# Feed-forward, second products: every engine in program order, casts a chunk ahead, border work over three chunks, side work in smaller pieces

## Chip, cores and metric

One NeuronCore of a Trainium2 chip runs the whole kernel. The metric is device microseconds (us) of one execution. The engines are TensorE (PE, matmuls; PEld are its weight loads), VectorE (DVE), ScalarE (ACT), GpSimd (POOL) and SyncE (SP, which issues nearly all transfers here). Each engine works through its own instructions in order and waits for others by semaphores.

## What is computed

One layer of a transformer-like block on 2048 tokens of width 1024, in fp32: attention and a gated branch, merged, and then the channel part that the change is about:

```python
    h2 = modulate(x, norm2_g[l], sh2, sc2)
    x = x + g2 * sq_relu_mlp(h2, w_ff1[l], w_ff2[l])

def sq_relu_mlp(h, w1, w2):
    return jnp.square(jax.nn.relu(h @ w1)) @ w2
```

The hidden width is 4096. The gate `g2` is 1024 columns of `silu(c) @ w_mod + b_mod`.

## The kernel before

Every fp32 product is made of three reduced matmuls: each operand is split into a high part h (a cast to fp32r by ACT) and a low part l (the value less its high part, by DVE), and `product` issues h·h, h·l and l·h (L1453, L1454, L1455), each 128x128 weights on 512 columns. The two big products of the feed-forward are in addition cut in two by two blocks and made by seven block products instead of eight (Strassen in Winograd's form), with sums formed by DVE.

The channel part comes last, in four stages; a block is 1024 tokens:

- `ff1` of block 0 (until about 2134 us): 16 groups of hidden columns. Each group makes seven products into PSUM banks, then ReLU and square by ACT (L1466, L1467), then the sums for the second product by DVE (L1463). The seven results of a group are stored to DRAM (`ao_d`), 256 KB each. Beside them `w2_ops` forms the seven sums of the second weights and stores them too (`w2o_d`, L1446).
- `ff2` of block 0 (about 2134 to 2463 us), the stage of the change: seven products p in the order 0, 1, 5, 6, 4, 2, 3, each in 8 chunks (NCH) of the hidden width. A step (p, c) is 24 matmuls: 4 token tiles (TT, one PSUM bank each) by 2 slots by 3. `ff2_chunk` loads a chunk of `ao_d` and one of `w2o_d` (512 KB each, L1542), lets ACT cast both (L1543) and DVE subtract (L1544); it is called two steps ahead of use.
- `ff1` and `ff2` of block 1 (to the end), alike, without `w2_ops`.

At the last chunk of a product, the **border**, `take` empties each bank: copies to SBUF by ACT (L1583, L1590), or `leave`: DVE multiplies with g2 and adds the residual (both through `tt`, L1556), and a later step issues the store to the output. For p = 1, ACT then writes an older sum back into the banks (L1586), since the next product adds onto it.

Beside `ff2` of block 0 runs **side work**, one piece per step: first the gate g2 (`mod_part`: 16 loads of weights, 16 DVE operations L364, L368, two matmuls L380), then `h_ops` for block 1, which prepares its `ff1` operands: load and scale a block of x (L1314, 128x2048 on DVE), 16 transposes by PE (L189), ACT scaling from PSUM (L1324), casts and subtractions (`halves`, L1298, L1299) and sums.

The order on an engine is not the program's. A scheduler reorders instructions by its costs and priorities, within the dependencies. `order` adds dependencies that hold some ranges: for `pins` every engine keeps program order, for `fixed` PE and DVE, for `loads` SP alone. Tiles of a tag are always given out in program order:

```python
            held = idx in pinned or (idx in fixed and i.engine in engines)
            held = held or (idx in loads and i.engine == self.nc.sync.engine)
```

Tags: b4 has 12 buffers of 512 KB, hb 35, f2 16 and f8 2. Before, a chunk takes four b4 buffers, so three chunks fit.

Of the kernel before, what the change touches and what calls it, by code (L numbers as in the profile page):

```python
# [11 lines left out]
F32R = mybir.dt.float32r  # L12
I32 = mybir.dt.int32
AF = mybir.ActivationFunctionType
ALU = mybir.AluOpType
# [4 lines left out]
P = 128  # L20
D = 1024
KC = D // P
# [8 lines left out]
TB = 512  # L31
# [20 lines left out]
def f32(ap):  # L52
    return ap.bitcast(F32)
# [17 lines left out]
class Kern:  # L71
# [280 lines left out]
    def mod_part(self, alloc, names):  # L352
        nc, I = self.nc, self.I
        for what in names:
            at = 2 * D + ("g1", "sh2", "sc2", "g2").index(what) * D
            for n in range(2):
                lo, sl = at + n * TB, slice(n * TB, (n + 1) * TB)
                acc = alloc()
                for k in range(KC):
                    w = alloc()  # L360
                    nc.sync.dma_start(w, I["w_mod"][0, k * P : (k + 1) * P, lo : lo + TB])
                    s = self.silu[:, k, 0:1]
                    if k == 0:
# [45 lines left out]
                yield  # L409

    def rope_consts(self):
        nc, I = self.nc, self.I
# [886 lines left out]
        nc.vector.tensor_tensor(out=l, in0=raw, in1=f32(h), op=ALU.subtract)  # L1299
        return h, l  # L1300

    def x1_block(self, blk, r, kk):
        nc, n = self.nc, 2 * TT
        x = self.sb("f8", [n, 2, P])
        for i in range(2):
            src = self.x1_d[2 * blk + i].rearrange("(t p) c -> p t c", p=P)
            for j in range(2):
                k = kk + j * HK
                nc.sync.dma_start(
                    x[:, i * TT : (i + 1) * TT, j], src[:, :, k * P : (k + 1) * P]  # L1310
                )
        xv = x.rearrange("p t j c -> p t (j c)")
        rb = r.unsqueeze(2).broadcast_to([P, n, 2 * P])
        nc.vector.tensor_tensor(out=xv, in0=xv, in1=rb, op=ALU.mult)  # L1314
        return x

    def x1_turned(self, x, kk):
        nc, raw = self.nc, {}
# [44 lines left out]
    def h_ops(self, blk, ops):  # L1363
        n = 2 * TT
        r = self.rsqrt(self.ss2[:, blk * n : (blk + 1) * n], n, 1.0 / D)
        add, sub = ALU.add, ALU.subtract
        tt = self.nc.vector.tensor_tensor
        for kk in range(HK):
# [145 lines left out]
    def ff1(self, blk, h, extra, w=None, late=()):  # L1514
# [5 lines left out]
        for g in range(NG):  # L1520
            nxt = iter(())
            if g + 1 < NG:
                w[g + 1] = {}
                nxt = self.w1_ops(g + 1, w[g + 1])
            else:
                self.ready = [self.ff2_chunk(blk, 0, 0)]
            more = extra(g)
            for _ in self.ff1_group(blk, g, w.pop(g), h):
                next(late, None)
# [4 lines left out]
            for _ in more:  # L1534
                pass

    def ff2_chunk(self, blk, p, c):
        nc = self.nc
        out = []
        for src in (self.ao_d[blk][p][c], self.wo_d[p][c]):  # L1540
            l, h = self.sb("b4", [2, TB], F32R), self.sb("b4", [2, TB], F32R)
            nc.sync.dma_start(f32(l), src.rearrange("s p c -> p s c"))  # L1542
            nc.scalar.copy(h, f32(l))  # L1543
            nc.vector.tensor_tensor(out=l, in0=f32(l), in1=f32(h), op=ALU.subtract)  # L1544
            out.append((h, l))
        return out

    def ff2(self, blk, side):
        nc = self.nc
        add, mult = ALU.add, ALU.mult  # L1550
        ready = self.ready + [self.ff2_chunk(blk, 0, 1)]
        begin = self.here()
        late = []

        def tt(out, in0, in1, op):
            nc.vector.tensor_tensor(out=out, in0=in0, in1=in1, op=op)  # L1556

        goes = {1: (0, 0), 4: (1, 1), 2: (0, 1), 3: (1, 0)}
        u2, u3, xs = ([None] * TT for _ in range(3))

        def residual(p):
            i, j = goes[p]
            for t in range(TT):
# [3 lines left out]
                    self.x1_d[2 * blk + i][t * P : (t + 1) * P, j * TB : (j + 1) * TB],  # L1567
                )

        def leave(p, t, src):  # L1570
            i, j = goes[p]
            row = (2 * blk + i) * TB + t * P
            cs = slice(j * TB, (j + 1) * TB)
            c = self.sb("f2", [TB])
            tt(c, src, self.g2b[:, cs], mult)
            tt(c, c, xs[t], add)
            late.append(lambda: nc.sync.dma_start(self.out[0, row : row + P, cs], c))

        def take(p, t):
            ps = banks[p][t]  # L1580
            if p == 0:
                u2[t] = self.sb("f2", [TB])
                nc.scalar.copy(u2[t], ps)  # L1583
            elif p == 1:
                leave(p, t, ps)
                nc.scalar.copy(ps, u2[t])  # L1586
            elif p in (5, 6):
                u = u2 if p == 5 else u3
                u[t] = self.sb("f2", [TB])
                nc.scalar.copy(u[t], ps)  # L1590
            elif p in (4, 2):
                u = u3[t] if p == 4 else u2[t]
                tt(u, u, ps, add)
                leave(p, t, u)
            else:
                leave(p, t, ps)

        order = (0, 1, 5, 6, 4, 2, 3)
        steps = [(p, c) for p in order for c in range(NCH)]
        banks = {}  # L1600
        for n, (p, c) in enumerate(steps):
            if n + 2 < len(steps):
                ready.append(self.ff2_chunk(blk, *steps[n + 2]))
            for f in late:
                f()
            late.clear()
            (ah, al), (wh, wl) = ready.pop(0)
            fresh = p in (0, 4)
            if c == 0 and fresh:
                new = [self.bank([TB]) for _ in range(TT)]  # L1610
                for other in (0, 1, 5, 6, 3) if p == 0 else (4, 2):
                    banks[other] = new
            if c == NCH - 1 and p in goes:
                residual(p)
            for t in range(TT):
                tok = slice(t * P, (t + 1) * P)
                a = [(ah[:, s, tok], al[:, s, tok]) for s in range(2)]
                b = [(wh[:, s], wl[:, s]) for s in range(2)]
                self.product(banks[p][t], a, b, fresh and c == 0)
                if c == NCH - 1:  # L1620
                    take(p, t)
            next(side, None)
        for f in late:
            f()
        for _ in side:
            pass
        self.loads.append(range(begin, self.here()))

    def ffn(self, h, w, w1, late):
        for _ in w1:  # L1630
# [6 lines left out]
        side = chain(self.mod_part(lambda: self.sb("f2", [TB]), ("g2",)), self.h_ops(1, h))  # L1637
        self.ff2(0, side)
        self.ff1(1, h, lambda g: iter(()))
        self.ff2(1, iter(()))  # L1640
# [449 lines left out]
```

## Time and profile before

| | before |
|---|---|
| median of 3 runs | 3111.57 us (3110.06 to 3111.89) |
| profiled execution | 3096.51 us, its span 3094.7 us |
| mean granted TensorE clock | 0.987 |
| PE, DVE, ACT, POOL busy | 2991.8, 2062.1, 1465.5, 688.6 us |
| HBM traffic | 172 GB/s over the span |

The profiled execution is 15 us shorter than the median of the runs. Busy time of PE counts pipelined matmuls with modelled ends, so a busy PE still may run slower than at full clock; the granted clock stands beside it for that. A row of the waits names what came last before an instruction could start. A timeline row has the start, the time taken, the engine (SPq is SP's queue), the line, the operation, and in brackets the idle time before it and what ended that.

### The profile page before, as it was taken

To read this page: it belongs to the slowest core of one execution; us is meant where nothing else is said; L and a number is where in the kernel's file an instruction comes from. 1 tells how busy PE (TensorE), PEld (TensorE's weight loads), DVE (VectorE), ACT (ScalarE), POOL (GpSimd) and SP (SyncE) were. 2 spreads that over 40 slices of the span, in tenths; PEclk is the share of its full clock that TensorE was granted. 3 is DMA by queue.
4 is the path that set the end of the run, shared out by engine and by line. 5 is a ranking of instruction groups with operands and counts; after the bars stand their busy time and mean duration, and the time that the engine had idled before them with its cause. 6 is when DMAs were issued, how large, how long until landed. Compare 5 with 4: busy or idle time off the path is not lost.

```text
span 3094.7 us, 37963 instructions
## 1 busy us (share of the span) xinstructions
PE 2991.8 (97%) x13501; PEld 2253.6 (73%) x13501; DVE 2062.1 (67%) x2918; ACT 1465.5 (47%) x2296; POOL 688.6 (22%) x506
## 2 busy tenths in 40 slices
PE   7999999979999999999999989999999999999999
PEld 4877788866555555556877878887777788888777
DVE  4776577866887777678654488776665566654445
ACT  5646664654554545554222255444454344444433
POOL 0000000002898888885234300000000000000000
PEclk8999999989999999999999999999999999999999
DMA  8686766643110000005855459887766644445665
GB/s 298 204 264 215 233 194 202 195 151 118 38 38 22 14 15 14 5 22 189 277 187 174 141 170 322 308 303 270 252 217 219 207 147 150 152 161 196 205 211 203
DMA packets 385726, 534.32 MB, mean 173 GB/s; under 512 B 32048, under 2 KB 203232, under 8 KB 385536
## 3 DMA queue, kind: packets, MB, share of 16 engines
q1 hardware_dynamic: 375760, 515.88, 50.3%
q10 hardware_dynamic: 9776, 16.01, 1.4%
q8 instruction: 106, 1.74, 0.2%
q14 instruction: 84, 0.69, 0.1%
HBM read 367.69 MB, written 164.10 MB: 172 GB/s over the span
## 4 chain that ended last, share of the span: by engine, by line
PE 78%; DMA 8%; DVE 6%; ACT 4%; issue 3%; POOL 1%; SPq 0%; DVEq 0%; ACTq 0%; POOLq 0%
PE b L1454 13%; PE b L1455 13%; PE b L1453 12%; PE b L1982 8%; PE b L1949 5%; PE b L1968 4%; PE b L1914 3%; PE a L1453 3%; PE b L183 3%; PE b L185 3%; PE a L1455 3%; PE a L1454 3%; PE b L184 3%; PE b L189 2%; DMA bw<-in_w_br_gm 1%
## 5 line engine op out<-in xcount | busy, mean ns | idle before, releaser
L1544 DVE TENSOR_TENSOR b<-b,b 128x1024 fp32r<-128x1024 f32 x224 | 272.9, 1223 | 241.1 <-ACT b L1543 236.3
L1925 DVE TENSOR_REDUCE ts<-b 128x1 f32<-128x512 f32 x512 | 314.7, 681 | 140.9 <-PE b L1914 140.9
L1543 ACT CAST b<-b 128x1024 fp32r<-128x1024 f32 x224 | 234.9, 1052 | 328.2 <-DMA b<-ao_d 290.7
L1454 PE MATMUL b<-b,b 128*128 128x512 f32 x896 | 351.4, 392 | 4.9 <-DVE b L1544 4.2
L1455 PE MATMUL b<-b,b 128*128 128x512 f32 x896 | 349.2, 390 | 0.0
L1453 PE MATMUL b<-b,b 128*128 128x512 f32 x896 | 308.3, 394 | 12.0 <-ACT b L1543 6.4
L1998 POOL TENSOR_TENSOR ac<-ac,p 128x512 f32<-128x512 f32 x216 | 301.5, 1428 | 66.2 <-ACT p L1972 65.4
L1972 ACT ACTIVATE p<-b 128x512 f32<-128x512 f32 x384 | 199.7, 616 | 164.9 <-PE b L1968 155.0
L1998 POOL TENSOR_TENSOR ac<-ac,t 128x512 f32<-128x512 f32 x152 | 217.6, 1456 | 0.0
L1453 PEld LDWEIGHTS b<-b,b 128*128 128x128 f32 x896 | 167.9, 188 | 54.4 <-ACT b L1543 11.3
L1454 PEld LDWEIGHTS b<-b,b 128*128 128x128 f32 x896 | 168.4, 188 | 46.8 <-DVE b L1544 12.4
L1949 PE MATMUL b<-h,h 128*128 128x512 f32 x576 | 199.8, 417 | 1.3 <-ACT p L1972 0.6
L1455 PEld LDWEIGHTS b<-b,b 128*128 128x128 f32 x896 | 168.5, 188 | 34.4
L1968 PE MATMUL b<-h,h 128*128 128x512 f32 x576 | 179.5, 393 | 0.0
L1982 PE MATMUL b<-p,h 128*64 128x512 f32 x768 | 175.3, 598 | 0.0
L1454 PE MATMUL b<-hb,b 128*128 128x512 f32 x448 | 174.6, 390 | 0.0
L1871 POOL MEMSET t<- 128x512 f32 x16 | 8.4, 525 | 696.2 <-DMA tb_d<-t 671.1
L1453 PE MATMUL b<-hb,b 128*128 128x512 f32 x416 | 162.1, 390 | 0.0
L1455 PE MATMUL b<-hb,b 128*128 128x512 f32 x416 | 161.5, 389 | 0.0
L1463 DVE TENSOR_TENSOR f<-f,b 128x512 f32<-128x512 f32 x160 | 109.1, 682 | 65.4 <-issue 43.0
L1949 PEld LDWEIGHTS b<-h,h 128*128 128x128 f32 x576 | 106.2, 189 | 58.5 <-DVE ts L1925 19.4
L1453 PE MATMUL a<-f,h 128*128 128x384 f32 (+1 forms) x320 | 117.5, 372 | 9.9 <-ACT f L607 4.7
(402 smaller groups left out, 6890.5 us busy)
## 6 DMA issues: line engine op xcount, KB each, us to landing
ao_d<-f SPq DMA_DIRECT2D x224, 256.0 KB
b<-ao_d SPq DMA_DIRECT2D x112, 512.0 KB
b<-w2o_d SPq DMA_DIRECT2D x112, 512.0 KB
f<-in_w_ff SPq DMA_DIRECT2D x48, 1024.0 KB
w2o_d<-f SPq DMA_DIRECT2D x112, 256.0 KB
f<-in_w_in SPq DMA_DIRECT2D x44, 512.0 KB
f<-x_d SPq DMA_DIRECT2D x64, 256.0 KB
m<-p_d SPq DMA_DIRECT2D x20, 512.0 KB
```

The source lines that it names most:

```text
L1453: mm(ps, wh, hh, start=start and k == 0, stop=False, skip_group_check=True)
L1454: mm(ps, wh, hl, start=False, stop=False, skip_group_check=True)
L1455: mm(ps, wl, hh, start=False, stop=k == len(w) - 1, skip_group_check=True)
L1463: nc.vector.tensor_tensor(out=out, in0=in0, in1=in1, op=op)
L1543: nc.scalar.copy(h, f32(l))
L1544: nc.vector.tensor_tensor(out=l, in0=f32(l), in1=f32(h), op=ALU.subtract)
L1925: nc.vector.tensor_reduce(out=self.mx[:, t, h, c : c + 1], in_=ps[h], axis=AX.X, op=ALU.max)
L1949: self.nc.tensor.matmul(self.pts[j][h], k.KA[c][self.kv][:, ks], self.qa[h], start=True, stop=False, skip_group_check=True,)
L1968: self.nc.tensor.matmul(s, k.KB[c][self.kv][:, ks], self.qb[h], start=False, stop=True, skip_group_check=True,)
L1972: self.nc.scalar.activation(pt[h], s, AF.Exp)
L1982: nc.tensor.matmul(self.o[h * HD : (h + 1) * HD, :], k.V[c][:, i, self.kv * HD : (self.kv + 1) * HD], pt[h], start=j == 0, stop=j == NKT - 1,)
L1998: nc.gpsimd.tensor_tensor(out=self.acc[e][:, h], in0=old[:, h], in1=pt[h], op=ALU.add)
```

## The change

1. The range of `ff2` goes from `loads` to `pins`: on every engine the instructions of the stage stand in program order. The first chunk's load and cast stay ahead of that range, in `ff1`; chunk 1, which stood ahead of the range too, is now inside.
2. `ff2_chunk` is split into `ff2_load`, called two steps ahead in block 0 and four in block 1, and `ff2_cast`, called one step ahead. In block 1 odd chunks go to 256 KB loads into hb tiles, each cast and subtracted by itself.
3. Border work is spread: residual loads two chunks earlier, for p = 4 and 2 the part `u*g2 + x` (`carried`, 8 DVE operations) a chunk before the end, the multiplication at the last chunk, the additions (`late`) one step on and the output stores (`stores`) another step on.
4. The gate is made by `last_gate`, which loads its weights a step ahead; `h_ops` loads the next block of x ahead. A side piece is called after token tile 1 of a step, in a product's last chunk after tile 3.

```diff
-            x = self.x1_block(blk, r, kk)
+            self.x1_scaled(x, r)
             yield
             raw = self.x1_turned(x, kk)
+            if kk + 1 < HK:
+                x = self.x1_load(blk, kk + 1)
             yield
...
-                self.ready = [self.ff2_chunk(blk, 0, 0)]
+                self.ready = [self.ff2_cast(self.ff2_load(blk, 0, 0))]
...
-        ready = self.ready + [self.ff2_chunk(blk, 0, 1)]
+        order = (0, 1, 5, 6, 4, 2, 3)
+        steps = [(p, c) for p in order for c in range(NCH)]
+        ahead = 4 if blk else 2
+
+        def load(n):
+            return self.ff2_load(blk, *steps[n], bool(blk) and n % 2 == 1)
+
         begin = self.here()
-        late = []
+        ready = self.ready
+        raws = [load(n) for n in range(1, ahead)]
+        late, stores = [], []
...
+        def carried(p):
+            _, cs = place(p)
+            for t in range(TT):
+                u = (u3 if p == 4 else u2)[t]
+                tt(u, u, self.g2b[:, cs], mult)
+                tt(xs[t], xs[t], u, add)
+
         def leave(p, t, src):
...
             tt(c, src, self.g2b[:, cs], mult)
-            tt(c, c, xs[t], add)
-            late.append(lambda: nc.sync.dma_start(self.out[0, row : row + P, cs], c))
+            lo = row + t * P
+
+            def rest():
+                tt(c, c, x, add)
+                stores.append(lambda: nc.sync.dma_start(self.out[0, lo : lo + P, cs], c))
+
+            late.append(rest)
...
         for n, (p, c) in enumerate(steps):
-            if n + 2 < len(steps):
-                ready.append(self.ff2_chunk(blk, *steps[n + 2]))
-            for f in late:
-                f()
-            late.clear()
-            (ah, al), (wh, wl) = ready.pop(0)
+            if n + ahead < len(steps):
+                raws.append(load(n + ahead))
+            flush(stores)
+            if raws:
+                ready.append(self.ff2_cast(raws.pop(0)))
+            flush(late)
+            a, b = ready.pop(0)
...
-            if c == NCH - 1 and p in goes:
+            if c == NCH - 3 and p in goes:
                 residual(p)
+            if c == NCH - 2 and p in (4, 2):
+                carried(p)
...
-            next(side, None)
-        for f in late:
-            f()
+                if t == (TT - 1 if c == NCH - 1 else 1):
+                    next(side, None)
+        flush(late)
+        flush(stores)
...
-        self.loads.append(range(begin, self.here()))
+        self.pins.append(range(begin, self.here()))
```

In `ff2_cast`, L1607 is the cast and L1608 the subtraction; L1595 are the 512 KB loads of `ff2_load`, L1592 the 256 KB ones, L1629 is `tt` in `ff2`, L1675 the copy back into the banks.

Three places show what the engines now have in another order. The first is SP's queue where `ff1` of block 0 ends and `ff2` of block 0 begins. Before (L1542 are the loads of chunks 1 and 2, the second number of `ao0_d0_1`; the other rows are `ff1`'s last stores, of which `ao0_d2_7` comes last):

```order
L1542 DMA b4_4163_18938<-ao0_d0_1_172 128x2x512
L1446 DMA w2o_d4_7_322<-f2_4151_18832 128x512
L1446 DMA w2o_d5_7_330<-f2_4152_18833 128x512
L1542 DMA b4_4165_18943<-w2o_d0_1_284 128x2x512
L1481 DMA ao0_d0_7_178<-f2_4155_18850 128x512
L1446 DMA w2o_d3_7_314<-f2_4154_18835 128x512
L1446 DMA w2o_d6_7_338<-f2_4153_18834 128x512
L1542 DMA b4_4167_18948<-ao0_d0_2_173 128x2x512
L1491 DMA ao0_d3_7_202<-f2_4158_18890 128x512
L1542 DMA b4_4169_18953<-w2o_d0_2_285 128x2x512
```

Now, the same place, the end of the stores and the first loads of the stage:

```order
L1551 DMA ao0_d6_7_226<-f2_4148_18814 128x512
L1559 DMA ao0_d1_7_186<-f2_4150_18830 128x512
L1560 DMA ao0_d2_7_194<-f2_4161_18933 128x512
L1595 DMA b4_4163_18938<-ao0_d0_1_172 128x2x512
L1595 DMA b4_4164_18940<-w2o_d0_1_284 128x2x512
L1595 DMA b4_4165_18942<-ao0_d0_2_173 128x2x512
L1595 DMA b4_4166_18944<-w2o_d0_2_285 128x2x512
L421 DMA g1_4162_18937<-in_b_mod 128x1024
L417 DMA f2_4173_18969<-in_w_mod 128x512
```

The loads of chunks 1 and 2 moved from among `ff1`'s last stores to behind the last of them.

The second place is DVE at the border after p = 1 in block 0 (b4 operands are chunks, `g1` is the buffer of the gate g2, and rows that read it are `leave`'s multiplications; the other rows of 512 columns with hb or f2 alone are side work). Before:

```order
L1544 TENSOR_TENSOR b4_4276_19592<-b4_4276_19592,b4_4277_19593 128x1024
L1556 TENSOR_TENSOR f2_4284_19616<-b_4171_18958,g1_4162_18937 128x512
L1544 TENSOR_TENSOR b4_4278_19597<-b4_4278_19597,b4_4279_19598 128x1024
L1556 TENSOR_TENSOR f2_4284_19616<-f2_4284_19616,f2_4280_19602 128x512
L1556 TENSOR_TENSOR f2_4285_19626<-b_4172_18959,g1_4162_18937 128x512
L1556 TENSOR_TENSOR f2_4286_19636<-b_4173_18960,g1_4162_18937 128x512
L1556 TENSOR_TENSOR f2_4285_19626<-f2_4285_19626,f2_4281_19604 128x512
L1556 TENSOR_TENSOR f2_4286_19636<-f2_4286_19636,f2_4282_19606 128x512
L1556 TENSOR_TENSOR f2_4287_19646<-b_4174_18961,g1_4162_18937 128x512
```

Now, from the multiplication for the last bank to the scaling of the next block of x (L1356):

```order
L1629 TENSOR_TENSOR f2_4290_19650<-b_4172_18955,g1_4162_18937 128x512
L1339 TENSOR_TENSOR hb_4292_19654<-f2_4267_19538,hb_4291_19653 128x512
L1433 TENSOR_TENSOR f2_4270_19541<-f2_4257_19489,f2_4268_19539 128x512
L1339 TENSOR_TENSOR hb_4294_19659<-f2_4255_19482,hb_4293_19658 128x512
L1339 TENSOR_TENSOR hb_4296_19663<-f2_4270_19541,hb_4295_19662 128x512
L1608 TENSOR_TENSOR b4_4283_19607<-b4_4283_19607,b4_4299_19670 128x1024
L1608 TENSOR_TENSOR b4_4284_19609<-b4_4284_19609,b4_4300_19673 128x1024
L1629 TENSOR_TENSOR f2_4287_19623<-f2_4287_19623,f2_4263_19518 128x512
L1629 TENSOR_TENSOR f2_4288_19632<-f2_4288_19632,f2_4264_19520 128x512
L1629 TENSOR_TENSOR f2_4289_19641<-f2_4289_19641,f2_4265_19522 128x512
L1629 TENSOR_TENSOR f2_4290_19650<-f2_4290_19650,f2_4266_19524 128x512
L1356 TENSOR_TENSOR f8_4258_19491<-f8_4258_19491,fs_4238_19374 128x2048
```

The four additions moved behind the multiplications, the pending side operations and the subtractions of chunk 17, and the scaling follows them.

The third place is DVE at the very end of block 1. Before, one addition followed its own multiplication:

```order
L1556 TENSOR_TENSOR f2_5191_25624<-b_4931_23644,g1_4162_18937 128x512
L1556 TENSOR_TENSOR f2_5191_25624<-f2_5191_25624,f2_5187_25610 128x512
L1556 TENSOR_TENSOR f2_5192_25633<-b_4932_23645,g1_4162_18937 128x512
L1556 TENSOR_TENSOR f2_5192_25633<-f2_5192_25633,f2_5188_25612 128x512
L1556 TENSOR_TENSOR f2_5193_25642<-b_4933_23646,g1_4162_18937 128x512
L1556 TENSOR_TENSOR f2_5194_25651<-b_4934_23647,g1_4162_18937 128x512
L1556 TENSOR_TENSOR f2_5193_25642<-f2_5193_25642,f2_5189_25614 128x512
L1556 TENSOR_TENSOR f2_5194_25651<-f2_5194_25651,f2_5190_25616 128x512
```

Now all four multiplications come first:

```order
L1629 TENSOR_TENSOR f2_5303_25919<-b_4939_23667,g1_4162_18937 128x512
L1629 TENSOR_TENSOR f2_5304_25927<-b_4940_23668,g1_4162_18937 128x512
L1629 TENSOR_TENSOR f2_5305_25935<-b_4941_23669,g1_4162_18937 128x512
L1629 TENSOR_TENSOR f2_5306_25943<-b_4942_23670,g1_4162_18937 128x512
L1629 TENSOR_TENSOR f2_5303_25919<-f2_5303_25919,f2_5295_25845 128x512
L1629 TENSOR_TENSOR f2_5304_25927<-f2_5304_25927,f2_5296_25847 128x512
L1629 TENSOR_TENSOR f2_5305_25935<-f2_5305_25935,f2_5297_25849 128x512
L1629 TENSOR_TENSOR f2_5306_25943<-f2_5306_25943,f2_5298_25851 128x512
```

The first output tile is complete only after the last bank has been multiplied.

More of the change, by code (lines that the diff above doesn't have):

```diff
@@ L409, in mod_part, with last_gate, fetch @@
                 yield
+    def last_gate(self):
+        nc, I = self.nc, self.I
+        def fetch(n, k):
+            lo = 5 * D + n * TB
+            w = self.sb("f2", [TB])
+            nc.sync.dma_start(w, I["w_mod"][0, k * P : (k + 1) * P, lo : lo + TB])
+            return w
+        steps = [(n, k) for n in range(2) for k in range(0, KC, 2)]
+        nc.sync.dma_start(
+            self.g2b, I["b_mod"][:, 5 * D : 6 * D].partition_broadcast(P)[:, 0, :]
+        )
+        ahead = [fetch(0, k) for k in range(2)]
+        yield
+        accs = []
+        for i, (n, k0) in enumerate(steps):
+            ws = ahead
+            if i + 1 < len(steps):
+                ahead = [fetch(steps[i + 1][0], steps[i + 1][1] + j) for j in range(2)]
+            if k0 == 0:
+                accs.append(self.sb("f2", [TB]))
+            for k, w in zip((k0, k0 + 1), ws):
+                s, acc = self.silu[:, k, 0:1], accs[n]
+                if k == 0:
+                    nc.vector.tensor_scalar(
+                        out=acc, in0=w, scalar1=s, scalar2=None, op0=ALU.mult
+                    )
+                else:
+                    nc.vector.scalar_tensor_tensor(
+                        out=acc, in0=w, scalar=s, in1=acc, op0=ALU.mult, op1=ALU.add
+                    )
+            yield
+        for n in range(2):
+            dst = self.g2b[:, n * TB : (n + 1) * TB]
+            ps = self.bank([TB])
+            nc.tensor.matmul(ps, self.ones, accs[n], start=True, stop=True)
+            nc.vector.tensor_tensor(out=dst, in0=ps, in1=dst, op=ALU.add)
+        yield
     def rope_consts(self):
@@ L1559, in ff2, with place @@
         u2, u3, xs = ([None] * TT for _ in range(3))
+        def place(p):
+            i, j = goes[p]
+            return (2 * blk + i) * TB, slice(j * TB, (j + 1) * TB)
         def residual(p):
@@ L1589, in take, with flush @@
                 u[t] = self.sb("f2", [TB])
                 nc.scalar.copy(u[t], ps)
[L1591 to L1594, printed above, removed]
             else:
                 leave(p, t, ps)
-        order = (0, 1, 5, 6, 4, 2, 3)
-        steps = [(p, c) for p in order for c in range(NCH)]
+                if p == 1:
+                    nc.scalar.copy(ps, u2[t])
+        def flush(fs):
+            for f in list(fs):
+                f()
+            fs.clear()
```

69 lines of the change are left out of this document (40 added, 29 removed).

## The prediction

> **What bounds the kernel now.** I read the head of the page, then the windows of the two stages that change, then the waits of PE, and last the timelines at the places where a wait ends. The head:
>
> ```profile
> span 3094.7 us, 37963 instructions
> PE 2991.8 (97%) x13501; PEld 2253.6 (73%) x13501; DVE 2062.1 (67%) x2918; ACT 1465.5 (47%) x2296; POOL 688.6 (22%) x506
> ```
>
> PE is busy for 97% of the span, and the change leaves its matmuls as they are. It can win only what PE loses in the second products. The windows around the two stages (columns: length, busy time of PE, PEld, DVE, ACT and POOL with counts, granted clock, share and rate of the transfers):
>
> ```profile
> 2080.00:2470.00 390.00, 376.61 (x1655) 304.45 (x1654) 242.69 (x271) 172.28 (x206) 0.00 (x0) 1.00 0.70 235
> 2740.00:3089.50 349.50, 342.93 (x1492) 278.42 (x1490) 171.60 (x169) 136.50 (x146) 0.00 (x0) 1.00 0.60 202
> ```
>
> PE is idle for 390.00 - 376.61 = 13.4 us around block 0's stage and for 6.6 us around block 1's. A lower clock is a second loss. Five-microsecond windows, the first two from an early stage:
>
> ```profile
> 375.00:380.00 5.00, 2.27 (x15) 2.08 (x14) 0.88 (x2) 0.58 (x1) 0.00 (x0) 0.88 0.85 338
> 380.00:385.00 5.00, 5.00 (x22) 3.83 (x22) 3.46 (x7) 1.79 (x3) 0.00 (x0) 0.78 0.85 250
> 2315.00:2320.00 5.00, 2.62 (x7) 1.75 (x7) 4.97 (x8) 4.68 (x8) 0.00 (x0) 0.76 0.95 319
> 2320.00:2325.00 5.00, 5.00 (x22) 4.09 (x21) 4.45 (x6) 3.16 (x3) 0.00 (x0) 0.90 0.83 311
> ```
>
> After an idle time of 2.73 us (5.00 - 2.27) the clock loses 0.12 x 5 + 0.22 x 5 = 1.7 us of work, and after that of 2.38 us at 2317 it loses 0.24 x 5 + 0.10 x 5 = 1.7 us again. So the two stages lose 13.4 + 6.6 + 1.7 = 21.7 us, and that is the most that can be won, 0.7%. What PE waits for, first from 2080 to 2470, then from 2740 (total, times, longest):
>
> ```profile
> PE b L1453 <- ACT b L1543: 4.7, 5, 2.4
> PE b L1453 <- ACT b L1586: 2.9, 2, 2.3
> PE b L1454 <- DVE b L1544: 2.5, 4, 1.0
> PE b L1453 <- DVE f L1463: 2.0, 1, 2.0
> ...
> PE b L1453 <- ACT b L1586: 2.4, 2, 1.7
> PE b L1453 <- ACT b L1543: 1.7, 4, 0.5
> PE b L1454 <- DVE b L1544: 1.6, 2, 1.0
> ```
>
> These are late casts and subtractions of chunks, the copies back into the banks at the border after p = 1, and one wait in `ff1`'s last group behind a chunk's subtraction.
>
> **The change part by part.** The durations that I use (last number before the bar of idle time: mean ns of one):
>
> ```profile
> L1544 DVE TENSOR_TENSOR b<-b,b 128x1024 fp32r<-128x1024 f32 x108 | 131.3, 1222 | 85.5 <-ACT b L1543 83.5
> L1543 ACT CAST b<-b 128x1024 fp32r<-128x1024 f32 x108 | 113.2, 1052 | 140.4 <-DMA b<-ao_d 122.2 <-DMA b<-w2o_d 11.8 <-DVE f L1556 5.0
> L1299 DVE TENSOR_TENSOR hb<-f,hb 128x512 fp32r<-128x512 f32 x17 | 11.0, 683 | 0.0
> L1298 ACT CAST hb<-f 128x512 fp32r<-128x512 f32 x17 | 9.9, 620 | 3.2 <-DVE f L1380 2.7 <-DVE f L1384 0.3
> L1314 DVE TENSOR_TENSOR f<-f,fs 128x2048 f32<-128x2048 f32 x4 | 9.2, 2290 | 5.2 <-DMA f<-x_d 5.2
> L1556 DVE TENSOR_TENSOR f<-b,g 128x512 f32<-128x512 f32 x8 | 5.3, 683 | 4.1 <-PE b L1455 4.1
> L1586 ACT COPY b<-f 128x512 f32<-128x512 f32 x4 | 2.4, 590 | 3.7 <-DVE f L1556 3.7
> L1466 ACT ACTIVATE f<-f 128x512 f32<-128x512 f32 x2 | 1.3, 630 | 1.4 <-DVE f L1463 1.4
> ```
>
> *The start of block 0's stage.* The timelines of SP and ACT show what stands there before, and a quiet place in block 1 for comparison (start, length; in brackets the idle time before and its end):
>
> ```profile
> 2133.83 0.39 PE L1455 MATMUL b<-hb,f 128*128 128x512 f32 x1
> 2134.05 0.39 PE L1453 MATMUL b<-b,b 128*128 128x512 f32 x1
> ...
> 2119.13 0.38 SPq L1542 DMA_DIRECT2D b<-ao_d  x1
> 2140.08 0.32 SPq L1511 DMA_DIRECT2D ao_d<-f  x1
> 2141.49 0.43 SPq L1542 DMA_DIRECT2D b<-w2o_d  x1
> 2149.03 1.05 ACT L1543 CAST b<-b 128x1024 fp32r<-128x1024 f32 x1 [0.23 <-DMA b<-w2o_d]
> ...
> 2801.26 0.36 SPq L1542 DMA_DIRECT2D b<-ao_d  x1
> 2801.71 0.42 SPq L1542 DMA_DIRECT2D b<-w2o_d  x1
> 2805.03 1.05 ACT L1543 CAST b<-b 128x1024 fp32r<-128x1024 f32 x1 [3.08 <-DMA b<-ao_d]
> 2806.51 1.05 ACT L1543 CAST b<-b 128x1024 fp32r<-128x1024 f32 x1 [0.44 <-DMA b<-w2o_d]
> ```
>
> Call T0 the time at which `ff1`'s last matmul gives way to step 0 (2134.05). Chunk 1 was loaded from 2119.13 on, 15 us ahead. Now its loads are queued on SP behind `ff1`'s last store, which waits for the end of a chain that starts with the sixth product, 12 matmuls of 0.227 us (from the two PE rows, 0.22) before T0, so at T0 - 2.7. The chain is add, ReLU, square, three sums, then for the seventh product add, ReLU, square and a last sum: six DVE operations at 0.68 or, back to back, about 0.60, and four of ACT at 0.63. With 0.25 for the last matmul's end that is T0 - 2.5 + 6.5 = T0 + 4.0. The store issues there, chunk 1's first load at T0 + 4.4, its second at T0 + 4.85. In the quiet place the second load's cast follows 4.80 us behind its issue, in the busy one at 2141.49 by 7.54 us. I take one us above the quiet one, since the stores before T0 still move: T0 + 10.65. Cast 1.05 and subtraction 1.22 end at T0 + 12.9; step 1 is due after 24 matmuls, at T0 + 5.44. PE waits 7.5 us, by the two rows 6.5 to 9.2. What hid these loads before was `ff1`'s last group; that cover is gone. Steps 2 to 5 follow from loads issued right behind and have 5.44 us each; I cost them at nothing, and bound this by 0 to 2. The wait of 2.0 us in `ff1` goes, as no chunk stands there.
>
> *The start of block 1's stage.* The queue has the same form. Chunk 1 is now four loads, the last issued at T0 + 5.75. With the quiet 3.77 us (2801.26 to 2805.03) and 0.5 above it, it lands at T0 + 10.0; cast 0.62, subtraction 0.68: T0 + 11.3. PE waits 5.9 us; if half the size lands a microsecond sooner 4.9, by the busy row 8.3.
>
> *The clock.* Idle times of 2.38 and 2.73 us each cost 1.7 us of clock. Two of 7.5 and 5.9 us cost 3.4, and before's 1.7 goes with its wait. Below 2.4 us the trace has a wait that cost none: at the border after p = 1, 2.3 us (the waits' second row) in
>
> ```profile
> 2220.00:2230.00 10.00, 6.99 (x28) 4.83 (x27) 9.62 (x12) 7.65 (x11) 0.00 (x0) 1.00 0.81 266
> ```
>
> The Trainium skill, TensorE: Matmul & The Clock Gate, Part 1, says that the clock halves after an idle window of about 3.4 us, free-running, and recovers after as long a busy one. The trace agrees on the loss (half of 3.4 is 1.7) but not on the idle time, of which 2.38 us did here; by the page alone before's drop would not be there and the sum would be 1.7 us higher.
>
> *The border after p = 1, block 0.* Call Te the end of step 15's matmuls. The last bank's multiplication ends at Te + 0.9, the copy back at Te + 1.5 (0.59). Behind it ACT and DVE take turns on the side work that now stands ahead of chunk 17: ACT's casts wait behind the copies, DVE's subtraction behind each cast, so four DVE operations end at about Te + 4.8, the casts of chunk 17 at Te + 6.1 and its second subtraction at Te + 7.3. Step 17 is due at Te + 5.44: 1.8 us. Then come four additions (2.4) and the scaling (2.29), at Te + 12.0, for transposes that stand behind two token tiles of step 17, at Te + 9.9: 2.1 us more. Together 3.9, against 3.6 before: 3.0 in the window just shown (10.00 - 6.99) and, of the 2.9 us on L1586, the 0.6 that its longest, 2.3, leaves. From below it is 0, if scheduling delays are shorter by 2 us at each; from above 6.
>
> *The other places.* Casts a chunk ahead remove the waits on L1543 and L1544: of block 0's 4.7 and 2.5 us I leave 1.5 where four ACT scalings stand ahead of a cast (2.4, the longest, before; 0 from below). At the border after p = 4, `carried`'s eight DVE operations (4.8 us) and two subtractions (2.3) pass a step by 1.7 us, of which the step in hand hides most: 0.5, from 0 to 1.7. Of block 1's 3.3 us I leave 0.2. The waits on L1586 in block 1 go, as the copy needs only the multiplication now. The gate's DVE operations stand behind loads issued a step earlier; a late load would hold the subtractions behind it, but the step has 5.44 us and DVE's chunk work 2.4, so nothing.
>
> *The end.*
>
> ```profile
> 3088.80 1.43 DVE L1556 TENSOR_TENSOR f<-b,g 128x512 f32<-128x512 f32 x2
> 3090.14 1.28 DVE L1556 TENSOR_TENSOR f<-f,f 128x512 f32<-128x512 f32 x2
> ```
>
> Before, two additions are left after the last multiplication, ending at 3091.42. Now four are: the multiplication ends at about 3090.3 and 0.69 + 3 x 0.60 = 2.5 later DVE ends, at 3092.8, and the last store starts 1.4 later (0 to 1.5).
>
> *The sum.* After: 7.5 + 5.9 + 3.4 + 3.9 + 1.5 + 0.5 + 0.2 = 22.9, with the end 24.3. Before 21.7. The change costs 2.6 us. The sum stands against the profiled execution of 3096.51 us (1.8 us outside its span), which lies 15 us under the median of 3111.57; I add it to the median: 3114.2 us. A difference of 0.2%, 6.2 us, is about what a measurement of this kernel can tell from none.
>
> **The rivals.** *Forecast, no change that can be measured (0.55):* the waits in the stages' middle go and come back at their starts. Its own range is 3108 to 3120.
>
> *Slower: transfers share the engines (0.20).* Behind chunk 1, SP issues chunk 2, the gate's bias and its first weights (together with chunk 1 about 3.1 MB), in block 1 three chunks (3.1 MB). If they are served together rather than in turn, chunk 1 is complete only when all are:
>
> ```profile
> 2140.00:2150.00 10.00, 10.00 (x46) 8.28 (x45) 2.45 (x5) 2.02 (x2) 0.00 (x0) 1.00 0.93 307
> ```
>
> 3.1 MB at 307 GB/s take 10 us. The waits become 4.85 + 10 + 2.27 - 5.44 = 11.7 and 5.75 + 10 + 1.3 - 5.44 = 11.6 us, 9.9 more: 3124 us. The busy pair (7.54 us) speaks for it, the quiet pair, whose second load comes behind its first, against. It decides from 1.8 us more than mine at each start.
>
> *Faster: the starts are short and the borders free (0.15).* Both starts at their lower bounds (-2.0), all borders and the ACT scalings at zero (-6.1), the end unchanged (-1.4): -9.5 against the forecast, 3104.7 us. It needs DVE to clear each border within its two steps; 97% of PE against 67% of DVE speaks for it, the order at the border against.
>
> That the change doesn't do what it says is excluded by the orders shown. 0.10 is left for waits that I have not seen, more of them losses, since in-order engines hand a late load on to all behind it.
>
> **The numbers.** Faster by over 0.2%: 0.13 of the faster rival, 0.03 of the rest: 0.16. Slower: 0.18 of the sharing, 0.07 of the rest, 0.07 of the forecast's upper end: 0.32. Within: 0.52. The range takes in both rivals' prices: 3104.5 to 3124.5.
>
> **What would show it.** Right: PE idle for 6 to 9 us at each stage's first step, ended by L1607 or L1608 of chunk 1, with the clock below 1 behind it; the first load of chunk 1 issued 4 to 5 us after T0; no 0.5 us waits on casts in block 1's middle; four additions after the last matmul. Wrong: no wait at the starts (then the time falls by 10 us and more), a load of chunk 1 that takes over 8 us, repeated waits in steps 2 to 6, or waits of over 6 us at the border after p = 1.

## The result, and the profile after

The changed kernel is faster. Its median is 3094.39 us (3091.73 to 3104.55, 10 runs) against 3106.53 us before (10 runs), and the ratio of the runs is 0.9974, with a 95% interval of 0.9963 to 0.9986: 4 to 12 us less. Forecast was 2.6 us more, 3114.2 us, and 3094.39 lies outside the range of 3104.5 to 3124.5. Part of that is the base: the three runs at hand had a median of 3111.57, ten have 3106.53. The rest is the sign. One execution among all the runs below, the profiled one of before_border, took 4093.9 us at a mean granted clock of 0.677, against 0.98 to 0.99 in the others, and stands in no ratio here.

The profiled execution of the changed kernel is longer than that of before, with a span of 3102.5 us against 3094.7:

```profile
span 3102.5 us, 38027 instructions
```

That says nothing on the change. Among the other executions profiled here the instructions that stand ahead of it, in one order in all kernels but for some operations of 128x8 and the last two on DVE and the last two transfers on SP, take up to 17 us more or less. So I compare from a matmul that lies ahead of the change: the 9300th of the list of PE's matmuls (counted from 0), 23 to 25 us before T0. Before and after it starts at

```profile
2108.66 0.39 PE L1454 MATMUL b<-hb,b 128*128 128x512 f32 x1
...
2122.10 0.39 PE L1503 MATMUL b<-hb,b 128*128 128x512 f32 x1
```

and the profiled execution after is already 13.4 us late there. From there to the end of the span, which I call the **stage**, before takes 3094.7 - 2108.7 = 986.1 us and after 3102.5 - 2122.1 = 980.4: 5.7 us less, inside the interval of the runs. The windows from that matmul to PE's last (before, then after):

```profile
2108.66:3089.50 980.84, 960.88 (x4202) 781.31 (x4200) 572.14 (x642) 429.29 (x523) 0.00 (x0) 1.00 0.59 198
...
2122.10:3096.02 973.92, 956.22 (x4202) 786.44 (x4200) 584.28 (x725) 423.74 (x578) 0.00 (x0) 0.99 0.58 199
```

The count of matmuls is the same. PE's idle time falls from 20.0 to 17.7 us, by only 2.3; its busy time falls by 4.7. This is the first sign that idle time does not carry the whole price of a wait. What PE waits for after, from 2080 and from 2740 on:

```profile
PE b L1502 <- ACT b L1607: 7.9, 3, 7.2
PE b L1503 <- DVE b L1608: 2.4, 3, 1.0
PE b L189 <- issue: 1.9, 1, 1.9
PE b L1502 <- DVE f L1629: 0.7, 1, 0.7
...
PE b L1502 <- ACT hb L1607: 4.9, 1, 4.9
```

Nine stops are left of 35 (idle times over 0.05 us), and two long ones are new, both at step 1. The timelines there, block 0 first (T0 is 2145.11):

```profile
2149.34 0.32 SPq L1560 DMA_DIRECT2D ao_d<-f  x1
2150.09 0.37 SPq L1595 DMA_DIRECT2D b<-ao_d  x1
2150.57 0.42 SPq L1595 DMA_DIRECT2D b<-w2o_d  x1
2156.76 1.05 ACT L1607 CAST b<-b 128x1024 fp32r<-128x1024 f32 x1 [0.29 <-DMA b<-w2o_d]
2157.86 0.80 PE L1502 MATMUL b<-b,b 128*128 128x512 f32 x1 [7.15 <-ACT b L1607]
2159.12 0.80 PE L1503 MATMUL b<-b,b 128*128 128x512 f32 x1 [0.46 <-DVE b L1608]
...
2793.61 0.79 PE L1502 MATMUL b<-hb,hb 128*128 128x512 f32 x1 [4.85 <-ACT hb L1607]
```

The load of chunk 1 is issued behind the last store, 5.0 us after T0, and PE stands for 7.6 us, in block 1 for 4.9. Behind each the clock is low:

```profile
2160.00:2165.00 5.00, 5.00 (x14) 3.90 (x14) 2.87 (x4) 0.39 (x1) 0.00 (x0) 0.54 1.03 390
2795.00:2800.00 5.00, 5.00 (x14) 3.87 (x13) 3.56 (x5) 3.87 (x6) 0.00 (x0) 0.55 1.05 399
```

The other new stops, at the border after p = 1 in block 0, and the end of the kernel:

```profile
2252.75 0.50 PE L1502 MATMUL b<-b,b 128*128 128x512 f32 x1 [0.40 <-ACT b L1607]
2254.20 0.50 PE L1503 MATMUL b<-b,b 128*128 128x512 f32 x1 [0.95 <-DVE b L1608]
2258.86 1.94 PE L189 MATMUL b<-ident,f 128*128 128x128 f32 x16 [1.87 <-issue]
...
3096.06 0.69 DVE L1629 TENSOR_TENSOR f<-b,g 128x512 f32<-128x512 f32 x1 [0.67 <-PE b L1504]
3096.67 2.49 DVE L1629 TENSOR_TENSOR f<-f,f 128x512 f32<-128x512 f32 x4
```

Nearly every term of what the changed kernel would lose is there, most of them in the forecast place. So I looked for the error in what before lost.

### The profile page after: what moved, and what is told of

It is laid out like the page before. It is cut to its first block, busy times and chain, and to the rows that moved or that the text cites. A ratio compares the mean times of both kernels' runs of the same rounds, so it can differ in the third digit from the quotient of the medians.

```text
span 3102.5 us, 38027 instructions
## 1 busy us (share of the span) xinstructions
PE 2994.0 (97%) x13501; PEld 2262.9 (73%) x13501; DVE 2074.6 (67%) x2990; ACT 1459.5 (47%) x2352; POOL 689.0 (22%) x506
## 4 chain that ended last, share of the span: by engine, by line
PE 83%; DMA 6%; DVE 5%; ACT 2%; issue 2%; POOL 1%; SPq 0%; ACTq 0%; DVEq 0%; POOLq 0%
PE b L1502 14%; PE b L1503 14%; PE b L1504 14%; PE b L2067 8%; PE b L2034 5%; PE b L2053 4%; PE b L183 3%; PE b L185 3%; PE b L184 3%; PE a L1502 3%; PE b L1999 3%; PE a L1503 3%; PE a L1504 3%; PE b L189 2%; DMA bw<-in_w_br_gm 1%
## 5 line engine op out<-in xcount | busy, mean ns | idle before, releaser
L1608 DVE TENSOR_TENSOR b<-b,b 128x1024 fp32r<-128x1024 f32 x168 | 198.6, 1221 | 145.0 <-ACT b L1607 144.6
L1607 ACT CAST b<-b 128x1024 fp32r<-128x1024 f32 x168 | 168.7, 1051 | 240.0 <-PE b L1503 222.0
L1502 PE MATMUL b<-b,b 128*128 128x512 f32 x672 | 263.9, 393 | 8.6 <-ACT b L1607 7.9
L1503 PE MATMUL b<-b,b 128*128 128x512 f32 x672 | 263.1, 391 | 2.4 <-DVE b L1608 2.4
L1504 PE MATMUL b<-b,b 128*128 128x512 f32 x672 | 262.6, 391 | 0.0
L1502 PEld LDWEIGHTS b<-b,b 128*128 128x128 f32 x672 | 126.9, 189 | 36.6 <-ACT b L1607 9.2
L1503 PEld LDWEIGHTS b<-b,b 128*128 128x128 f32 x672 | 126.8, 189 | 30.0 <-DVE b L1608 3.7
L1504 PEld LDWEIGHTS b<-b,b 128*128 128x128 f32 x672 | 126.8, 189 | 26.5
```

Source lines behind the costliest of these rows:

```text
L1502: mm(ps, wh, hh, start=start and k == 0, stop=False, skip_group_check=True)
L1503: mm(ps, wh, hl, start=False, stop=False, skip_group_check=True)
L1504: mm(ps, wl, hh, start=False, stop=k == len(w) - 1, skip_group_check=True)
```

## Experiments

Two questions: what does a stop cost, and which part of the change does the work? The table has the ratio of the runs to those of before with its interval and, from one profiled execution each, the length of the stage. The last two columns are PE's stops and the idle time in them, counted from the matmul ahead of the last twelve of block 0's `ff1` on.

| kernel | ratio, 95% interval | stage, us | idle, us | stops |
|---|---|---|---|---|
| before | 1 | 986.1 | 19.9 | 35 |
| after | 0.9974 (0.9963 to 0.9986) | 980.4 | 17.7 | 9 |
| c1_loads | 0.9923 (0.9909 to 0.9936) | 966.4 | 8.4 | 10 |
| c1_casts | 0.9923 (0.9910 to 0.9936) | 965.0 | 7.6 | 10 |
| loads_only | 0.9936 (0.9919 to 0.9952) | 968.3 | 11.1 | 2 |
| before_pins | 1.0015 (1.0007 to 1.0024) | 992.8 | 27.4 | 22 |
| c1_free | 0.9912 (0.9895 to 0.9929) | 961.1 | 4.7 | 5 |
| free_adds_at_once | 0.9910 (0.9891 to 0.9928) | 960.4 | 4.8 | 5 |
| free_old_side | 0.9903 (0.9886 to 0.9919) | 957.2 | 3.4 | 4 |
| free_c2 | 0.9935 (0.9915 to 0.9955) | 967.8 | 8.1 | 7 |
| stops_b1 | 1.0035 (1.0024 to 1.0046) | 998.7 | 29.7 | 42 |
| before_casts | 0.9916 (0.9897 to 0.9935) | 959.7 | 4.9 | 6 |
| casts_slots | 0.9905 (0.9888 to 0.9922) | 959.3 | 4.1 | 5 |
| before_border | 1.0034 (1.0019 to 1.0048) | no usable trace | | |

**c1_loads: the waits at the starts.**

```diff
                 self.ready = [self.ff2_cast(self.ff2_load(blk, 0, 0))]
+                self.raws = [self.ff2_load(blk, 0, 1)]
...
-        raws = [load(n) for n in range(1, ahead)]
+        raws = self.raws + [load(n) for n in range(2, ahead)]
```

> The changed kernel with one edit: in both blocks the loads of chunk 1 are issued in ff1, behind chunk 0's, ahead of the last group's stores (block 1's chunk 1 as two 512 KB loads); casts as in the change. Theory 1 (the waits at the starts come from the place in SP's queue): step 1 of block 0 no longer waits for a load but for the casts behind ff1's last activations, an idle time of 1 to 1.5 us instead of 7.6, in block 1 about 1 instead of 4.9; with the clock drops gone the kernel is 12 to 16 us faster than the changed kernel, some 18 to 22 under the one before. Theory 2 (the transfers' rate is the limit there): the wait moves to steps 2 to 5 and less than 5 us is won.

The stage shortens by 13.9 us against the changed kernel, as theory 1 has it. What is left at step 1 is 0.95 us of idle on a subtraction in each block, and another 0.64 at step 3 of block 0 and step 2 of block 1. Theory 2, transfers that share the engines, was also the slower rival of the prediction; it falls. Idle time fell by 9.3 us, the stage by 14. The low clock went too: the granted clock stays at 1 in the stage until PE's last matmul has ended.

**c1_casts: the casts ahead as well.**

```diff
-                self.ready = [self.ff2_cast(self.ff2_load(blk, 0, 0))]
+                self.ready = [self.ff2_cast(self.ff2_load(blk, 0, c)) for c in range(2)]
...
-        raws = [load(n) for n in range(1, ahead)]
+        raws = [load(n) for n in range(2, ahead)]
...
-            if raws:
+            if raws and n:
```

> As the kernel with chunk 1's loads moved, and chunk 1's casts and subtractions are issued in ff1 too, where the scheduler places them among the last group's work. Theory 1: no wait at step 1, but a wait of up to 2 us in ff1's last group in block 0, as before the change; within 2 us of the kernel with only the loads moved. Theory 2: as there, less than 5 us won against the changed kernel.

965.0 us, within 1.4 of the kernel above. The wait in `ff1` that I expected did not come.

**loads_only: without program order on PE, DVE and ACT.**

```diff
-        self.pins.append(range(begin, self.here()))
+        self.loads.append(range(begin, self.here()))
```

> The changed kernel with the range of ff2 held on SP alone (loads instead of pins), all else as changed. If program order on ACT, DVE and PE is what removes the many small waits (each costing more than the idle time that the profile shows), they come back: 6 or more stops of 0.5 us idle per block and a time like that of the kernel before or 3 to 8 us above the changed kernel. If the split of casts and border work removes them, the time is within 3 us of the changed kernel.

Neither: the kernel is faster than the changed one, with a stage 12.1 us shorter. Its waits:

```profile
PE b L1502 <- ACT b L1607: 6.6, 1, 6.6
PE b L1502 <- ACT hb L1607: 4.4, 1, 4.4
```

Only the two starts are left. All other stops, the 3.2 us of idle at the border after p = 1 among them, are made by program order, not removed by it.

**before_pins: program order alone.** The same line changed the other way, in the kernel before.

> The kernel before with only the hold changed: ff2's range is held in program order on all engines, chunk 1 stays ahead of it. If program order alone gives the gain, 5 to 10 us faster than before. If casts a chunk ahead and split border work are needed for it, casts that stand ahead of border work but wait for loads hold the engines: equal to before or slower by up to 20 us.

6.7 us longer in the stage, 0.15% in time. The part of the change named first in it is a loss by itself.

**stops_b1: what a stop costs.** In c1_loads, a cast is tied to PE in block 1:

```diff
-            if raws:
+            if raws and not (blk and n):
                 ready.append(self.ff2_cast(raws.pop(0)))
...
                 self.product(banks[p][t], at, b, fresh and c == 0)
+                if blk and n and t == 1 and raws:
+                    nc.scalar.copy(self.sb("f2", [TB])[:, :16], banks[p][t][:, :16])
+                    ready.append(self.ff2_cast(raws.pop(0)))
```

> The kernel with early loads and everything in program order, with a stop put into nearly every step of block 1: after the matmuls of token tile 1 ACT copies 16 columns of its bank and only then casts the next chunk, so that its subtractions end about 1 us behind the step's end. Some 50 stops. Theory 1 (a stop costs more than the idle time that the profile shows, since the last matmul's modelled end hides 0.16 us and the next ones start slower): block 1's stage grows by the idle time that the trace shows plus 0.25 to 0.55 us a stop, 13 to 27 us more than idle. Rival (idle time is the whole price): growth and idle agree within 3 us.

The windows of block 1 between the same two matmuls, of c1_loads and of stops_b1, and the waits of the second:

```profile
2754.66:3074.35 319.69, 318.10 (x1402) 262.69 (x1400) 164.37 (x216) 126.78 (x188) 0.00 (x0) 1.00 0.58 207
```

```profile
2759.62:3111.78 352.16, 329.61 (x1401) 258.63 (x1400) 165.85 (x216) 132.16 (x242) 0.00 (x0) 1.00 0.53 188
...
PE b L1503 <- DVE b L1609: 19.1, 28, 0.9
PE b L1503 <- DVE hb L1609: 3.3, 4, 1.4
```

Idle time grows by (352.16 - 329.61) - (319.69 - 318.10) = 21.0 us, the stretch by 32.5, at an undisturbed clock. c1_loads has two waits there, this kernel 32: each new one costs 11.5 / 30 = 0.38 us beyond its idle time. Fewer stops came than expected (every second step has none), but the price per stop is inside theory 1's bounds, and the rival is out. One stop in PE's timeline:

```profile
2796.74 0.39 PE L1502 MATMUL b<-b,b 128*128 128x512 f32 x1
2797.79 0.50 PE L1503 MATMUL b<-b,b 128*128 128x512 f32 x1 [0.66 <-DVE b L1609]
2798.12 0.39 PE L1504 MATMUL b<-b,b 128*128 128x512 f32 x1
```

From start to start 1.05 + 0.33 us pass where 2 x 0.227 would: 0.93 lost, 0.66 shown as idle. A matmul takes 0.39 us at a pace of 0.227, so 0.16 of every stop counts as busy, and the matmul that restarts takes 0.50, with the next 0.33 behind it.

**c1_free: both gains together.** The edits of c1_loads and loads_only.

> Chunk 1's loads in ff1 and, besides, ff2's range held on SP alone. If the two gains are independent (starts: -13.8 us in the stage's length by the traces; scheduler free in the middle and at the end: -12.1), the stage from the matmul 9300 on to the end of the span takes about 955 us against 980.4 of the changed kernel and 966.4 with the loads alone, and the kernel runs at about 3075 us. If the free scheduler won only at the starts, it stays within 2 us of the kernel with the loads alone.

961.1 us and a ratio of 0.9912: 5.3 us in the stage beyond c1_loads, 6 short of the sum. About that much, 5.9 us from start to start with the low clock behind it, is lost at a stop that the changed kernel doesn't have, in block 0's step 3 (a cast that waited for its load accounts for 0.93 us of idle there, the wait in the last row below for 2.74):

```profile
2157.86 1.54 DVE L440 SCALAR_TENSOR_TENSOR f<-f,silu,f 128x512 f32<-128x512 f32 x2 [2.63 <-DMA f<-in_w_mod]
2159.31 2.35 DVE L1609 TENSOR_TENSOR b<-b,b 128x1024 fp32r<-128x1024 f32 x2
...
2161.72 0.80 PE L1503 MATMUL b<-b,b 128*128 128x512 f32 x1 [2.74 <-DVE b L1609]
```

DVE stands idle until a weight of the gate has landed, and the chunk's subtractions are queued behind that.

**free_adds_at_once and free_old_side: border and side work undone.** In c1_free, `rest()` in place of `late.append(rest)`; and `mod_part`, `x1_block` and one piece at the end of each step as before the change.

> As the kernel with early loads and the free scheduler, with one part of the border's split undone: each addition follows its multiplication at once. If the spreading of border work carries the gain, DVE again holds the subtractions at the borders: 1 to 3 stops more per block, 3 to 8 us slower. If the earlier casts carry it, within 2 us of it; the end 1 us shorter, since two additions are left after the last matmul and not four.

> As the kernel with early loads and the free scheduler, with the side work as before the change: gate by mod_part, block x loaded in the step that scales it, one piece at the end of each step. If the side work's split carries the gain in block 0, the stops at the transposes come back there (0.5 to 2.4 us idle each, 5 to 8 us in all) and block 1 is unchanged; if not, within 2 us.

Additions at once: 960.4 against 961.1 us, no difference; the end is no shorter either, since the scheduler had already mixed them. Old side work: 3.9 us shorter in the stage, all in block 0; the intervals of the runs overlap (0.9903 and 0.9912). The new side work does not carry a gain here.

**free_c2: chunk 2's loads ahead too.** In free_old_side:

```diff
-                self.raws = [self.ff2_load(blk, 0, 1)]
+                self.raws = [self.ff2_load(blk, 0, c) for c in (1, 2)]
...
-        ahead = 4 if blk else 2
+        ahead = 4 if blk else 3
...
-        raws = self.raws + [load(n) for n in range(2, ahead)]
+        raws = self.raws + [load(n) for n in range(3, ahead)]
```

> The kernel with early loads, free scheduler and the old side work, and in addition chunk 2's loads ahead of ff1's last stores (three steps ahead in block 0). If the remaining stops at the starts (0.6 and 2.5 us lost at steps 1 and 2 of block 0, 0.9 and 0.7 in block 1) come from chunk 2's place in the queue, the stage shortens by 2 to 3 us to about 954.5; if from the casts' order on ACT and DVE, it stays at 957.

Wrong: 10.5 us longer than free_old_side. The stops at steps 1 and 2 stay, and in block 0 the scaling of x waits 6.8 us for its load, so that PE stands for 3.7 us ahead of transposes. Whether the earlier chunk loads delay that load or its place in the queue does was not tried.

**before_casts: the casts alone.** In the kernel before, `ff2_chunk` split; loads two steps ahead as they were, casts one:

```diff
             if n + 2 < len(steps):
-                ready.append(self.ff2_chunk(blk, *steps[n + 2]))
+                raws.append(self.ff2_load(blk, *steps[n + 2]))
+            if n and raws:
+                ready.append(self.ff2_cast(raws.pop(0)))
```

> The kernel before with one part of the change alone: loads still two steps ahead, casts and subtractions issued one step ahead of use (chunk 1's still in ff1). Hold, border work and side work as before. If the place of the casts carries the gain, its many small stops on casts and subtractions go and the stage takes 960 to 970 us against 986.1 of before; if the border work carries it, within 5 us of before.

26.4 us shorter, 0.84% (0.65 to 1.03) in time: this part does more than the whole change. At the border after p = 0 in block 1, ACT's timeline before and in this kernel:

```profile
2810.43 1.05 ACT L1543 CAST b<-b 128x1024 fp32r<-128x1024 f32 x1 [2.86 <-DMA b<-ao_d]
2814.41 0.59 ACT L1583 COPY f<-b 128x512 f32<-128x512 f32 x1 [2.93 <-PE b L1455]
2815.55 0.59 ACT L1583 COPY f<-b 128x512 f32<-128x512 f32 x1 [0.55 <-PE b L1455]
2816.68 0.59 ACT L1583 COPY f<-b 128x512 f32<-128x512 f32 x1 [0.55 <-PE b L1455]
2817.16 1.05 ACT L1543 CAST b<-b 128x1024 fp32r<-128x1024 f32 x1
```

```profile
2804.79 2.01 ACT L1553 CAST b<-b 128x1024 fp32r<-128x1024 f32 x2 [3.44 <-PE b L1454]
2806.70 0.58 ACT L1593 COPY f<-b 128x512 f32<-128x512 f32 x1
2807.74 0.59 ACT L1593 COPY f<-b 128x512 f32<-128x512 f32 x1 [0.46 <-PE b L1455]
2809.10 0.59 ACT L1593 COPY f<-b 128x512 f32<-128x512 f32 x1 [0.77 <-PE b L1455]
2810.23 1.05 ACT L1553 CAST b<-b 128x1024 fp32r<-128x1024 f32 x1 [0.55 <-PE b L1454]
```

Before, the cast of the weights that the next step needs stands behind three copies that wait for PE's banks one by one, and PE then waits for it:

```profile
2817.39 0.39 PE L1455 MATMUL b<-b,b 128*128 128x512 f32 x1
2818.26 1.19 PE L1453 MATMUL b<-b,b 128*128 128x512 f32 x4 [0.49 <-ACT b L1543]
2819.52 0.50 PE L1454 MATMUL b<-b,b 128*128 128x512 f32 x1
2819.86 0.39 PE L1455 MATMUL b<-b,b 128*128 128x512 f32 x1
```

Now both casts of that chunk stand ahead of the copies, and what stands among the copies is due a step later. The whole stop before is two restarts, and costs 1.1 us for 0.55 of idle.

**casts_slots: the place or the buffers?** A high part that is given out a step later also leaves two of the twelve b4 buffers free, so loads could start earlier. Here both buffers of a chunk are given out at the load:

```diff
-            l = self.sb("b4", [2, TB], F32R)
+            l, h = self.sb("b4", [2, TB], F32R), self.sb("b4", [2, TB], F32R)
```

> The kernel before with casts issued one step ahead of use, as in the run with the casts alone, but with both buffers of a chunk (raw and high part) given out when its load is issued, so that three chunks hold all twelve b4 buffers as before and a load still waits for the end of the step three chunks earlier. If the later place of the casts in program order is what counts, the stage takes 957 to 963 us like the run with the casts alone. If the buffers count (a chunk whose high part is given out late leaves two free, so that loads start a step earlier and a cast has a step in hand when ACT stands behind border copies), the gain is gone: 980 to 988 us, with the stops of 0.5 us idle on L1543's casts back.

959.3 us: the place of the casts counts, not the buffers. Why the scheduler puts one cast fewer ahead of the copies when the program has the casts earlier follows from its own costs, which I did not examine.

**before_border: the border work alone.** The kernel before with `carried`, residual loads at NCH - 3 and additions and stores a step later each.

> The kernel before with the border's part of the change alone: residual loads two chunks earlier, the carried sum a chunk earlier, additions and stores a step on each; casts two steps ahead and side work as before. If the border work carries the gain, the stops on the copies back after p = 1 and at the later borders go (3.6 us idle in block 0, 2.4 in block 1 and some of the others) and the stage takes 970 to 976 us; if only the casts do, 980 to 986.

Slower by 0.34% (0.19 to 0.48), some 10 us. There is no trace of it that can be set beside the others, so where it loses is open; that this part carries no gain by itself is shown.

**The parts together.** In the stage, the casts' place takes 986.1 us to 959.7 (before_casts), a gain of 26.4. With the border work, the side work and block 1's split loads it is 961.1 (c1_free), 1.4 more. With chunk 1's loads late and every engine in program order it is 980.4 (after), 19.3 more. What is left is the gain of 5.7.

## Why the prediction was wrong, by its steps

**The step that failed is the first sum: what before loses.** I took 21.7 us: idle time from the windows, and 1.7 of clock. With 0.38 us beyond idle for each of 35 stops it is 19.9 + 13.3 + 1.7 = 35 us. Sums over PE's starts agree. I took every matmul, from the one ahead of `ff1`'s last twelve on, that starts more than 0.3 us behind one of 512 columns, and added what lies above a pace of 0.227: 33.5 us in all, the clock included. In the changed kernel the same sum is 27.2. So more than a third of what could be won was missed, and "21.7 us is the most that can be won" was false: free_old_side wins 29 in the stage. The page itself says that a matmul's end is modelled and that busy time is not time at peak; I quoted the busy share and did not use that.

**What after loses was nearly right.** At the start of block 0: idle 7.6 us (7.5 forecast), of block 1 4.9 (5.9). At the border after p = 1, 3.9 us from start to start (3.9 forecast; the terms, 1.8 and 2.1, come as 0.40 + 0.95 and 1.87 of idle). The border after p = 4 costs 0.9 (0.5), the end 1.25 (1.4). Two of these fits are luck in part. At block 0's start the cast of chunk 1 ended at T0 + 12.7, 1.0 us later than forecast; from start to start 8.3 us are lost, of which 7.6 show as idle. And the 1.5 us that I left for a cast behind ACT's scalings came as 1.9 us at another place, step 27, where the cast stands behind one of the side work (L1338) that waited 2.09 us for DVE. With 9 stops at 0.38 and the clock, the loss is 17.7 + 3.4 + 5.8 = 26.9 us against 22.9.

**The clock's price was too low.** Not 1.7 but about 2.9 us at each start. The low clock lasts from the restart at 2157.9 to about 2164.7, and in block 1 from 2793.6 to about 2799.6 (the rows of 0.54 and 0.55): 6.8 and 6.0 us, where it was 3.4 after before's stop at 2317. The Trainium skill, TensorE: Matmul & The Clock Gate, Part 1, has the clock come back after a busy window of about 3.4 us that is free-running. From that I estimate that up to twice as long, 6.8 us, can pass behind a restart, and the trace agrees with its 6.8 and 6.0 us.

**The sum made right.** 26.9 + 1.25 against 35 is -6.9 us, where the stages differ by -5.7 and the runs by -4 to -12. Even with the forecast's own 22.9 for what after loses, 3.4 for its nine stops and 1.4 for the end, the 35 would have given -7.3 us: a gain, as measured.

**Rivals.** "Transfers share the engines" (0.20) did not happen: the second load's cast came 6.2 us after its issue, between the two rows quoted. "Faster" (0.15) has the right sign for a wrong reason: it needed short starts and free borders, and there were neither. The late load of a gate weight, costed at nothing, does hold the subtractions in c1_free, for 2.7 us of PE's idle time. In the changed kernel PE has no such stop; that the wait at the start gives those loads the time to land is my reading, not shown. One part that I never priced apart was the scheduler's freedom; giving it up costs 12.1 us (loads_only against after), which the casts' later place outweighs.

## What to carry to other kernels

Count what a bound engine loses from the starts of its instructions, not from its idle time: many short stops can cost twice what they show. Price the parts of a change one by one: here one part, casts put one step before use instead of two, wins 0.84%, while program order on all engines (0.15%) and the rearranged border work (0.34%) each lose when put into the kernel before. Before a range is held in order, look at which loads fall behind the work that ends the stage before it: moving one chunk's loads in each block back ahead of that work won 14 us.

Nine of these versions beat both kernels. The lowest are free_old_side (0.9903), casts_slots (0.9905), free_adds_at_once (0.9910), c1_free (0.9912) and before_casts (0.9916). Their intervals overlap, and which is best is open.

## What I had not expected of the hardware

In the stops shown, a stop of PE costs 0.27 us beyond its idle time when one restart ends it and 0.55 when PE restarts twice; over 30 stops it was 0.38 on average.

After a stop of 7.6 us the clock stayed at half for 6.8 us, after one of 4.9 for 6.0, after one of 2.4 for about 3.4. The length of a stop alone does not tell whether the clock falls: in before, 2.26 us at 2229 cost none, while in before_pins a stop of 1.87 us at 2445 was enough (granted clock 0.66 from 2445 to 2450).

And instructions in all but the same order, with no part in the change, take up to 17 us more or less from one execution to another (the 9300th matmul starts between 2108.7 and 2126.0 us). That is three times the 5.7 us that the change is worth in the stage, so a span says little here where a stage says much.
